# Heads' stage by a plan: when queries and keys are prepared and where the filling products stand

## The chip, the cores and the metric

The kernel runs on one core of a Trainium2 chip. The metric is the device time of one execution in microseconds (us). The engines are TensorE (PE; its weight loads are shown apart as PEld), VectorE (DVE), ScalarE (ACT), GpSimd (POOL) and SyncE (SP), whose queue issues the DMAs.

## The reference, cut to what matters

Two layers over 512 latent tokens and 256 context tokens of width 1024. The first mixes tokens by grouped-query attention with 16 heads of width 64 and 4 key/value heads; the second is a Mamba-2 mixer. Each is followed by a gated feed-forward network. The change touches the attention alone:

```python
q_l, k_l, v_l = jnp.split(h_lat @ w_qkv, [Q_DIM, Q_DIM + KV_DIM], axis=-1)
q_l = rms_norm(q_l.reshape(bsz, seq, N_HEADS, HEAD_DIM), q_norm)
k_l = rms_norm(k_l.reshape(bsz, seq, N_KV_HEADS, HEAD_DIM), k_norm)
q_l = apply_rope(q_l, cos, sin)
k_l = apply_rope(k_l, cos, sin)
...
s = jnp.einsum('bqhgd,bkhd->bhgqk', q, k).astype(jnp.float32) * (HEAD_DIM ** -0.5)
p = jax.nn.softmax(s, axis=-1).astype(v.dtype)
return jnp.einsum('bhgqk,bkhd->bqhgd', p, v)
```

Context queries see context keys only. `q`, `k` and `v` also exist for the context; there is no rotation for it. Besides, each layer has a modulation (shift, scale, gate) from a matrix product with the conditioning vectors.

## The kernel before

All of it is float32. Products of large matrices are made from a high and a low half of each operand: `split` casts the high half on ACT and subtracts on DVE or POOL for the low half, and `mm3` makes three products (high by high, high by low, low by high).

The attention goes through these stages. First the projections of keys and of the first four pairs' queries from slabs of weights (`ps_l`, `ps_c`). Then the *values' stretch*: `values()` makes the value products `ps_v`, 48 small steps. Between them stand the maxima of pair 0 and the preparation of pair 1's queries. Then the *heads' stage*: 16 heads in 8 pairs.

A pair (`class Pair`) has two parts. `maxima` multiplies queries by keys once for the row maxima (`ps_m`, reduced on DVE, `ma`, `mb`), and ends with their minima of the negated values `mz` and a diagonal `diag`. `steps` has seven steps: scores into `ps_s` (with the diagonal, which subtracts the maxima), an exponential on ACT into `pr`, a running sum on DVE (`acc`, `accc`). The value products `ps_o` and `ps_oc` come one step later, with the sum (`ps_sum`) and its reciprocal by logarithm and exponential (`final`). During the steps of a pair stands the `maxima` of the next. `ps_s` and `ps_m` share two buffers, so PE can run ahead of ACT and DVE by about a step.

A *preparation* (`normed`, in `queries` or `keys`) makes a pair's queries, or two key heads, ready. It squares and scales on ACT, sends four small DMAs that swap rows (`qsw`), rotates by three products on POOL (L534 to L536), sums columns on PE (`ssq`), makes a row scale on DVE and ACT (`rsa`, `rsy`, `rsu`, `rbq`), transposes it on PE (`rsTq`), multiplies it in on DVE (L540), and splits.

*Filling products* stand between the steps so that PE has work while the other engines follow. Those are the query projections of pairs 4 to 7 (`ps_q`), which a preparation follows, and six modulations (`ada`, `ps_ada`). `Fill.run` gives each step 1.75 us of them, from a list of generators in the order `123a4k5a6a7aaa` (digits: queries, with projection and preparation in one generator; k: the second keys; a: a modulation). After a `BREAK` a generator rests three steps and the next in the list goes on. What the next pair needs and isn't ready, `fill.require` forces at the pair's start. Weights are loaded when a generator starts. In pairs 6 and 7 the fill is the output projection (`ps_d`).

Each engine works its own queue in order. The program's order is not the queue's order in full: a scheduler places each instruction by its own estimate of when it is ready.

```python
adas = list(fill.q)
fill.q = [kgen if o == "k" else adas.pop(0) if o == "a" else qgen[int(o)] for o in "123a4k5a6a7aaa"]
...
    if p < 7:
        fill.require(qgen[p + 1])
        if p == 3:
            fill.require(kgen)
        m = pairs[p + 1].maxima()
    us = 1.75 if p < 6 else 2.9
```

Of the kernel before, what the change touches and what calls it, by code (L numbers as in the profile page):

```python
# [7 lines left out]
P = 128  # L8
F32 = mybir.dt.float32
F32R = mybir.dt.float32r  # L10
# [6 lines left out]
KT = D // P  # L17
L = 512
C = 256
# [48 lines left out]
def t3(g, name, dt=F32, n=T):  # L68
    return g.t3p.tile([P, n], dt, tag="t3", bufs=g.n3, name=name)


def t4(g, name, dt=F32):
    return g.p.tile([P, 1024], dt, tag="t4", bufs=10, name=name)


def _r(ap):

    return ap.bitcast(F32)


def split(g, src, hi, lo, lo_engine="dve", pin=False):

    nc = g.nc
    keep = g.tc.keep_in_program_order if pin else lambda i: i
    keep(nc.scalar.copy(hi, src))  # L85
    eng = nc.vector if lo_engine == "dve" else nc.gpsimd
    keep(eng.tensor_tensor(lo, src, _r(hi), ALU.subtract))  # L87


def load_w(g, dram, lo_engine="dve", pin=False):  # L90

    st = t4(g, "wst")
    wh = t4(g, "wh", F32R)
    wl = t4(g, "wl", F32R)
    g.nc.sync.dma_start(st, dram)
    split(g, st, wh, wl, lo_engine=lo_engine, pin=pin)
    return wh, wl


def mm3(g, w, outs, first, last):  # L100

    wh, wl = w
    mm = g.nc.tensor.matmul
    for out, (ah, al) in outs:
        mm(out, wh, ah, start=first, stop=False)  # L105
        mm(out, wh, al, start=False, stop=False)  # L106
    for out, (ah, al) in outs:
        mm(out, wl, ah, start=False, stop=last)  # L108
# [64 lines left out]
BREAK = object()  # L173
# [128 lines left out]
def S(g, name):  # L302
    return g.ps.tile([P, 1024], F32, tag="S", bufs=2, name=name)


def Bank(g, name):
    return g.ps.tile([P, 512], F32, tag="B", bufs=4, name=name)
# [72 lines left out]
def attention(g, fill, X, late):  # L380


    nc, I = g.nc, g.I
    S64 = slice(0, 64), slice(64, 128)
    Bk, Sb = (lambda name: Bank(g, name)), (lambda name: S(g, name))
    t2 = lambda name, dt=F32: g.t3p.tile([P, 512], dt, tag="t2", bufs=6, name=name)
    g.h = [[htiles(g, n, f"a{i}_{m}") for m in range(KT)] for i, n in enumerate((L, C))]
    hl, hc = g.h
# [58 lines left out]
    e = g.p.tile([P, 2 * KT], F32, name="silu")  # L447
# [8 lines left out]
    rsl, _, _ = next(norm)  # L456
# [12 lines left out]
    for m in range(KT):  # L469
# [14 lines left out]
        if m == 4:  # L484
            rsc = t3(g, "rsc", n=C)
            pt, _, _ = next(norm)
# [20 lines left out]
    raw = [t3(g, f"raw{j}") for j in range(6)]  # L507
# [18 lines left out]
    def normed(qs, gain, eng):  # L526

        sq = t3(g, "qsq")
        nc.scalar.activation(sq, qs, AF.Square)
        nc.scalar.activation(qs, qs, AF.Identity, scale=gain)  # L530
        sw = t2("qsw")
        for b in range(4):
            nc.sync.dma_start(sw[32 * (b ^ 1) : 32 * (b ^ 1) + 32], qs[32 * b : 32 * b + 32, :L])
        eng.tensor_tensor(qs[:, :L], qs[:, :L], g.cos, ALU.mult)  # L534
        eng.tensor_tensor(sw, sw, g.sin, ALU.mult)
        eng.tensor_tensor(qs[:, :L], qs[:, :L], sw, ALU.add)  # L536
        for r in rstd_rows(g, sq, T, g.blk, HD, "q", Bk):
            if r is not BREAK:
                pt, c0, c1 = r
                nc.vector.tensor_tensor(qs[:, c0:c1], qs[:, c0:c1], pt[:, : c1 - c0], ALU.mult)  # L540
            yield BREAK
# [3 lines left out]
    def keys(j, qs, eng):  # L545
        yield from normed(qs, kn, eng)
        nat = t3(g, f"kh{j}", F32R), t3(g, f"kl{j}", F32R)
        swp = t3(g, f"khs{j}", F32R), t3(g, f"kls{j}", F32R)
        split(g, qs, *nat)
        for a, b in zip(swp, nat):  # L550
            for e in range(2):
                nc.sync.dma_start(_r(a)[S64[e]], _r(b)[S64[1 - e]])
        k2[2 * j], k2[2 * j + 1] = (nat, swp), (swp, nat)
        yield 0

    qprep = {}

    def queries(p, qs, eng):
        if qs is None:
            w = load_w(g, I["wq"][p - 4], lo_engine="pool")  # L560
            yield BREAK
            qs = t3(g, "qs")
            for h, c0, n in ((hc, L, C), (hl, 0, L)):
                ps = Bk("ps_q")
                for k in range(KT):
                    ks = slice(k * P, (k + 1) * P)
                    mm3(g, (w[0][:, ks], w[1][:, ks]), [(ps[:, :n], h[k])], k == 0, k == KT - 1)
                    yield 3 * n / 2400
                nc.scalar.copy(qs[:, c0 : c0 + n], ps[:, :n])
            yield BREAK  # L570
        yield from normed(qs, g.qn8, eng)
        qprep[p] = t3(g, "qh", F32R), t3(g, "ql", F32R)
        split(g, qs, *qprep[p])
        yield 0
# [8 lines left out]
    class Pair:  # L583
# [43 lines left out]
        def steps(self):  # L627
# [61 lines left out]
                    lambda pr=pr, acc=acc: later_ctx(pr, acc))  # L689
            g.o.append(o)  # L690

    early = [keys(0, raw[0], nc.vector), queries(0, raw[1], nc.vector)]
    for n, j in enumerate((0, 1, 2, 4, 5, 3)):
        ps = Bk("ps_c")
        for k in range(KT):
# [7 lines left out]
    for gen in early:  # L703
        for _ in gen:
            next(vals)
            next(vals)
    qgen = {p: queries(p, raw[{1: 2, 2: 4, 3: 5}[p]] if p < 4 else None, nc.gpsimd) for p in range(1, 8)}
    kgen = keys(1, raw[3], nc.gpsimd)

    g.oT = []  # L710
# [2 lines left out]
    def osplit(p):  # L713
        hl_, hc_ = htiles(g, L, f"ol{p}"), htiles(g, C, f"oc{p}")
        o = g.o[p]
        if p < 6:
            o = t3(g, f"od{p}")
            nc.sync.dma_start(o, odram[p])
        split(g, o[:, :L], *hl_)
        split(g, o[:, L:T], *hc_)  # L720
        g.oT.append((hl_, hc_))

    adas = list(fill.q)
    fill.q = [kgen if o == "k" else adas.pop(0) if o == "a" else qgen[int(o)] for o in "123a4k5a6a7aaa"]
    g.o = []
    pairs = [Pair(p) for p in range(NH // 2)]

    m = pairs[0].maxima()
    for i, _ in enumerate(vals):
        if i % 5 == 2:  # L730
            next(m, None)
        if i % 6 == 5:
            next(qgen[1], None)
    for _ in m:
        pass
    late_step = None
    for p in range(NH // 2):
        m = iter(())
        if p < 7:
            fill.require(qgen[p + 1])  # L740
            if p == 3:
                fill.require(kgen)
            m = pairs[p + 1].maxima()
        us = 1.75 if p < 6 else 2.9
        for t, todo in enumerate(pairs[p].steps()):
            next(m, None)
            if late_step:
                late_step()
            late_step = todo
            if t == 0:  # L750
                if p == 6:
                    for i in range(5):
                        osplit(i)
                    late()
            if p == 7 and t == 3:
                osplit(5)
                osplit(6)
            fill.run(us)
    late_step()
    osplit(7)  # L760

# [490 lines left out]
def body(nc, tc, I, out, dbg=None):  # L1252
# [47 lines left out]
    def late():  # L1300
        for fs in ((0, 1, 2), (3, 4), (5, 6, 7))[:-1]:
            fill.add(project(fs))

    attention(g, fill, X, late)
    fill.drain()
    g.tables = True
# [133 lines left out]
```

## Time and profile before

| | |
|---|---|
| median of 3 runs | 1893.8 us (1892.28 to 1894.25) |
| profiled execution | 1893.6 us, span 1891.8 us, mean granted PE clock 0.997 |
| PE, DVE, ACT, POOL busy | 98%, 70%, 43%, 16% of the span |
| heads' stage, pairs 0 to 5 | from 107.8 to 295.6 us of the span |
| values' stretch | up to 107.8 us |

The profile's lines give start and length in us, the engine, the line in the code, the operation, what it writes and reads, and the shapes. In brackets stand the idle time before an instruction and the instruction that ended it. Matmuls are pipelined and their ends are modelled, so a busy PE is not yet a PE at full rate; the distance from one start to the next says more.

### The profile page before, as it was taken

What the parts mean: (1) busy time and instruction counts of PE and PEld (TensorE: products, weight loads), DVE (VectorE), ACT (ScalarE), POOL (GpSimd) and SP (SyncE); (2) the same over time, 40 slices, a digit from 0 to 9 for tenths busy, and PEclk for the clock granted to TensorE, in tenths of its full rate; (3) what the DMA queues carried; (4) which work ended last, traced back from release to release, by engine and by line L of the source; (5) the groups of instructions that cost most, each with busy time, mean ns of one, the idle gap of its engine ahead of it and who ended that gap; (6) DMA issues with size and microseconds to landing.
All of it is one profiled execution on the core that took longest, in us unless ns stands there. A gap on an engine that the chain in (4) does not pass through costs nothing.

```text
span 1891.8 us, 28789 instructions
## 1 busy us (share of the span) xinstructions
PE 1859.4 (98%) x11474; PEld 1548.3 (82%) x11474; DVE 1314.9 (70%) x1950; ACT 811.4 (43%) x1410; POOL 302.8 (16%) x266
## 2 busy tenths in 40 slices
PE   9999999999999999999999999999999999999999
PEld 7866565688888888888888888888887888888887
DVE  6587778687877776444487877777787476565655
ACT  4544443364222222222366676776666252323331
POOL 2231120040000000000041334444333210000000
PEclk9999999999999999999999999999999999999999
DMA  9322341115443553112224323333453222323232
GB/s 342 91 95 62 132 156 37 34 57 190 145 134 131 180 182 123 65 67 68 67 90 125 114 92 116 118 120 126 123 158 106 72 91 100 100 83 107 90 100 89
DMA packets 74070, 211.67 MB, mean 112 GB/s; under 512 B 9040, under 2 KB 14544, under 8 KB 73808
## 3 DMA queue, kind: packets, MB, share of 16 engines
q1 hardware_dynamic: 73936, 209.84, 33.5%
q8 instruction: 90, 1.47, 0.3%
q14 instruction: 44, 0.36, 0.1%
HBM read 198.79 MB, written 6.82 MB: 109 GB/s over the span
## 4 chain that ended last, share of the span: by engine, by line
PE 80%; DVE 11%; issue 3%; DMA 2%; ACT 2%; POOL 1%; SPq 0%; DVEq 0%; POOLq 0%; ACTq 0%
PE ps_up L108 10%; PE ps_up L106 10%; PE ps_up L105 10%; PE ps_d L105 6%; PE ps_d L106 6%; PE ps_d L108 6%; PE ps_in L108 4%; PE ps_in L106 4%; PE ps_in L105 4%; PE ps_o L636 2%; PE ps_s L672 2%; PE ps_st L1030 2%; DVE ht L281 1%; DVE wl L87 1%; PE ps_wo L108 1%
## 5 line engine op out<-in xcount | busy, mean ns | idle before, releaser
L87 DVE TENSOR_TENSOR wl<-wst,wh 128x1024 fp32r<-128x1024 f32 x207 | 260.4, 1258 | 229.3 <-PE ps_up L106 133.0
L85 ACT CAST wh<-wst 128x1024 fp32r<-128x1024 f32 x211 | 221.1, 1049 | 396.4 <-DMA wst<-in_wup 321.5
L106 PE MATMUL ps_up<-hlf,wh 128*128 128x512 f32 (+1 forms) x1008 | 357.0, 354 | 0.0
L108 PE MATMUL ps_up<-hhf,wl 128*128 128x512 f32 (+1 forms) x1008 | 356.8, 354 | 0.0
L105 PE MATMUL ps_up<-hhf,wh 128*128 128x512 f32 x1008 | 356.8, 354 | 0.0
L106 PEld LDWEIGHTS ps_up<-hlf,wh 128*128 128x128 f32 x1008 | 190.7, 189 | 26.3
L105 PEld LDWEIGHTS ps_up<-hhf,wh 128*128 128x128 f32 x1008 | 190.5, 189 | 26.5
L108 PEld LDWEIGHTS ps_up<-hhf,wl 128*128 128x128 f32 x1008 | 190.5, 189 | 26.3
L105 PE MATMUL ps_in<-hhs,wh 128*128 128x512 f32 (+1 forms) x560 | 204.4, 365 | 1.2 <-ACT dt L915 1.2
L106 PE MATMUL ps_in<-hls,wh 128*128 128x512 f32 (+1 forms) x560 | 199.4, 356 | 0.0
L108 PE MATMUL ps_in<-hhs,wl 128*128 128x512 f32 (+1 forms) x560 | 198.7, 355 | 0.0
L105 PE MATMUL ps_d<-hdh,wh 128*128 128x512 f32 (+1 forms) x568 | 193.5, 342 | 0.2 <-ACT hdh L85 0.2
L108 PE MATMUL ps_d<-hdh,wl 128*128 128x512 f32 (+1 forms) x568 | 193.5, 341 | 0.0
L106 PE MATMUL ps_d<-hdl,wh 128*128 128x512 f32 (+1 forms) x568 | 192.9, 340 | 0.3 <-DVE hdl L87 0.3
L781 DVE SCALAR_TENSOR_TENSOR X<-ps_d,mod,X 128x512 f32<-128x512 f32 (+1 forms) x224 | 124.8, 587 | 35.2 <-PE ps_d L108 35.0
L105 PEld LDWEIGHTS ps_in<-hhs,wh 128*128 128x128 f32 x560 | 105.9, 189 | 16.3 <-ACT dt L915 1.4
L106 PEld LDWEIGHTS ps_d<-hdl,wh 128*128 128x128 f32 x568 | 106.7, 188 | 14.8 <-DVE hdl L87 0.7
L108 PEld LDWEIGHTS ps_in<-hhs,wl 128*128 128x128 f32 x560 | 105.8, 189 | 14.8
L108 PEld LDWEIGHTS ps_d<-hdh,wl 128*128 128x128 f32 x568 | 106.7, 188 | 13.1
L105 PEld LDWEIGHTS ps_d<-hdh,wh 128*128 128x128 f32 x568 | 106.3, 188 | 13.6 <-ACT hdh L85 0.7
L106 PEld LDWEIGHTS ps_in<-hls,wh 128*128 128x128 f32 x560 | 106.0, 189 | 13.2
L675 ACT ACTIVATE pr<-ps_s 128x1024 f32<-128x1024 f32 x56 | 57.2, 1022 | 108.8 <-PE ps_s L674 106.5
(344 smaller groups left out, 3682.8 us busy)
## 6 DMA issues: line engine op xcount, KB each, us to landing
wst<-in_wup SPq DMA_DIRECT2D x88, 512.0 KB, 3.3
wada<-in_adaT SPq DMA_DIRECT2D x56, 512.0 KB, 3.3
wst<-in_win SPq DMA_DIRECT2D x48, 512.0 KB, 3.4
wst<-in_wdown SPq DMA_DIRECT2D x44, 512.0 KB, 3.9
E<-ad SPq DMA_DIRECT2D x64, 256.0 KB, 6.4
wada<-in_adaB SPq DMA_DIRECT2D x24, 512.0 KB, 4.0
ec<-ead SPq DMA_DIRECT2D x64, 128.0 KB, 5.1
wst<-in_wout SPq DMA_DIRECT2D x16, 512.0 KB, 3.3
```

What stands on the lines that cost most here:

```text
L85: keep(nc.scalar.copy(hi, src))
L87: keep(eng.tensor_tensor(lo, src, _r(hi), ALU.subtract))
L105: mm(out, wh, ah, start=first, stop=False)
L106: mm(out, wh, al, start=False, stop=False)
L108: mm(out, wl, ah, start=False, stop=last)
L281: nc.vector.scalar_tensor_tensor(t[:, c0:c1], ap, g.moda[layer][ca][:, m, v : v + 1], rs[:, c0:c1], ALU.mult, ALU.mult)
L636: nc.tensor.matmul(po[S64[e], :n], v, pr[:, 512 * e + off : 512 * e + off + n], start=first, stop=last)
L672: nc.tensor.matmul(outs[e], kk[e][a][S64[e], k], b[S64[e], q], start=i == 0, stop=False)
L675: nc.scalar.activation(pr, ps, AF.Exp)
L781: nc.vector.scalar_tensor_tensor(ap, o[:, c0:c1], gate[:, m, v : v + 1], ap, ALU.mult, ALU.add)
L1030: nc.tensor.matmul(ps[:, d * 256 : (d + 1) * 256], Bt[:, t * P : (t + 1) * P], xw[d][t], start=t == ts[0], stop=t == ts[-1])
```

## The change

The heads' stage is laid out by a plan. Projection (`qproj`) and preparation (`queries`) of a pair's queries are now two generators. One preparation is done in each pair of heads: `prep` = queries of pair 3, second keys, queries of pairs 4 to 7, at least a pair ahead of their use, at fixed steps (0, 3, 4, 5, rest at 6). Pairs and steps count from 0. The third queries, those of pair 2, are prepared in the values' stretch, beside pair 1's. The fill comes from one stream, `a4a567aaaa`, in shares of 1.04 us a step, with the DMA of an item sent two items ahead and the split of its weights one item ahead. A modulation's rest follows two steps after its products. From pair 6 on nothing is changed.

```diff
-    def queries(p, qs, eng):
-        if qs is None:
-            w = load_w(g, I["wq"][p - 4], lo_engine="pool")
-            yield BREAK
-            qs = t3(g, "qs")
...
+    def qproj(p):
+        st = t4(g, "wst")
+        nc.sync.dma_start(st, I["wq"][p - 4])
+        yield
+        w = t4(g, "wh", F32R), t4(g, "wl", F32R)
+        split(g, st, *w, lo_engine="pool")
+        yield
+        qs = qraw[p] = t3(g, "qs")
...
+    def queries(p, eng):
+        qs = qraw[p]
         yield from normed(qs, g.qn8, eng)
...
-    fill.q = [kgen if o == "k" else adas.pop(0) if o == "a" else qgen[int(o)] for o in "123a4k5a6a7aaa"]
+    items = [adas.pop(0) if o == "a" else qproj(int(o)) for o in "a4a567aaaa"]
+    tails = []
+    def stream():
+        for it in items[:2]:
+            next(it)
+        yield
+        for i, it in enumerate(items):
+            if i + 2 < len(items):
+                next(items[i + 2])
+            if i + 1 < len(items) and i + 1 in (1, 3, 4, 5):
+                next(items[i + 1])
+            if i in (1, 3, 4, 5):
+                yield from it
+            else:
+                next(it)
+                tails.append([2, it])
+                yield 1.95
...
+    prep = {0: qgen[3], 1: kgen, 2: qgen[4], 3: qgen[5], 4: qgen[6], 5: qgen[7]}
...
         if i % 6 == 5:
             next(qgen[1], None)
+        if i in (12, 26, 30, 34):
+            next(qgen[2], None)
+        if i == 20:
+            next(side)
...
-            fill.run(us)
+            if p < 6:
+                if t in (0, 3, 4, 5):
+                    next(prep[p])
+                if t == 6:
+                    for _ in prep[p]:
+                        pass
+                spread(1.04)
+            else:
+                fill.run(2.9)
```

What it moves, at three places. PE in pair 0, from its first maxima on, before:

```order
L236 MATMUL ssq<-cst,qsq 128x2 x6
L672 MATMUL ps_s<-qh,kh_1139 128x512
...
L600 MATMUL ps_m<-khs_1141,qh 128x512
L236 MATMUL ssq<-cst,qsq 128x2 x6
L636 MATMUL ps_o<-pr,v_910 64x512 x2
L129 MATMUL ps_ada<-wada,sc_83 32x128 x32
```

and after:

```order
L236 MATMUL ssq<-cst,qsq 128x2 x6
L129 MATMUL ps_ada<-wada,sc_83 32x128 x32
L680 MATMUL ps_s<-qh,kh_1139 128x512
...
L608 MATMUL ps_m<-khs_1141,qh 128x512
L644 MATMUL ps_o<-pr,v_910 64x512 x2
L105 MATMUL ps_q<-hha_0_118,wh 128x256
L106 MATMUL ps_q<-hla_0_119,wh 128x256
L108 MATMUL ps_q<-hha_0_118,wl 128x256
```

One preparation's column sums stand there in place of two, and the query products start in the second step.

POOL at the same place (`raw4` and `raw5` are the raw queries of pairs 2 and 3, `raw3` the second keys, `wl` a low half of query weights), before:

```order
L87 TENSOR_TENSOR wl_1571<-wst_1569,wh_1570 128x1024
L536 TENSOR_TENSOR raw4_902<-raw4_902,qsw_1454 128x512
L87 TENSOR_TENSOR wl_1623<-wst_1621,wh_1622 128x1024
L534 TENSOR_TENSOR raw5_903<-raw5_903,cs_74 128x512
L535 TENSOR_TENSOR qsw_1482<-qsw_1482,cs_74 128x512
L536 TENSOR_TENSOR raw5_903<-raw5_903,qsw_1482 128x512
L534 TENSOR_TENSOR raw3_901<-raw3_901,cs_74 128x512
```

and after:

```order
L534 TENSOR_TENSOR raw5_903<-raw5_903,cs_74 128x512
L535 TENSOR_TENSOR qsw_1506<-qsw_1506,cs_74 128x512
L536 TENSOR_TENSOR raw5_903<-raw5_903,qsw_1506 128x512
L87 TENSOR_TENSOR wl_1540<-wst_1351,wh_1539 128x1024
L87 TENSOR_TENSOR wl_1893<-wst_1597,wh_1892 128x1024
L87 TENSOR_TENSOR wl_1983<-wst_1890,wh_1982 128x1024
L534 TENSOR_TENSOR raw3_901<-raw3_901,cs_74 128x512
```

Three low halves now stand in a row ahead of the second keys' rotation; before, the third came after it.

PE in pair 5, from its first value products (before) and from its first preparation product (after). Before:

```order
L636 MATMUL ps_o<-pr,v_910 64x512 x2
L129 MATMUL ps_ada<-wada,sc_83 32x128 x32
...
L636 MATMUL ps_o<-pr,v_911 64x512 x2
L236 MATMUL ssq<-cst,qsq 128x2 x6
...
L636 MATMUL ps_o<-pr,v_913 64x512 x2
L253 MATMUL rsTq<-cst,rbq 128x128 x4
```

and after:

```order
L236 MATMUL ssq<-cst,qsq 128x2 x6
L129 MATMUL ps_ada<-wada,sc_83 32x128 x32
...
L644 MATMUL ps_o<-pr,v_911 64x512 x2
L129 MATMUL ps_ada<-wada,sc_83 32x128 x32
...
L644 MATMUL ps_o<-pr,v_912 64x512 x2
L253 MATMUL rsTq<-cst,rbq 128x128 x4
L129 MATMUL ps_ada<-wada,sc_83 32x128 x32
```

The last preparation's column sums move ahead by two steps, and three modulations, of which two stood together at the pair's start, are spread to steps 0, 2 and 3. The last three steps hold no modulation in either.

More of the change, by code (lines that the diff above doesn't have):

```diff
@@ L556, in attention @@
     qprep = {}
-    def queries(p, qs, eng):
-        if qs is None:
-            w = load_w(g, I["wq"][p - 4], lo_engine="pool")
-            yield BREAK
-            qs = t3(g, "qs")
[L563 to L570, printed above, removed]
+    qraw = {p: raw[j] for p, j in ((0, 1), (1, 2), (2, 4), (3, 5))}
+    def qproj(p):
[6 more added lines that the diff above has]
+        qs = qraw[p] = t3(g, "qs")
+        for h, c0, n in ((hc, L, C), (hl, 0, L)):
+            ps = Bk("ps_q")
+            for k in range(KT):
+                ks = slice(k * P, (k + 1) * P)
+                mm3(g, (w[0][:, ks], w[1][:, ks]), [(ps[:, :n], h[k])], k == 0, k == KT - 1)
+                yield 3 * n / 2400
+            nc.scalar.copy(qs[:, c0 : c0 + n], ps[:, :n])
+    def queries(p, eng):
+        qs = qraw[p]
         yield from normed(qs, g.qn8, eng)
@@ L690, in steps @@
             g.o.append(o)
-    early = [keys(0, raw[0], nc.vector), queries(0, raw[1], nc.vector)]
+    early = [keys(0, raw[0], nc.vector), queries(0, nc.vector)]
     for n, j in enumerate((0, 1, 2, 4, 5, 3)):
@@ L706, in attention @@
             next(vals)
-    qgen = {p: queries(p, raw[{1: 2, 2: 4, 3: 5}[p]] if p < 4 else None, nc.gpsimd) for p in range(1, 8)}
+    qgen = {p: queries(p, nc.gpsimd) for p in range(1, 8)}
     kgen = keys(1, raw[3], nc.gpsimd)
@@ L721, in osplit, with spread @@
         g.oT.append((hl_, hc_))
-    adas = list(fill.q)
-    fill.q = [kgen if o == "k" else adas.pop(0) if o == "a" else qgen[int(o)] for o in "123a4k5a6a7aaa"]
+    adas, fill.q = list(fill.q), []
+    items = [adas.pop(0) if o == "a" else qproj(int(o)) for o in "a4a567aaaa"]
[15 more added lines that the diff above has]
+                yield 1.95
+    def spread(us):
+        nonlocal owed
+        for e in list(tails):
+            e[0] -= 1
+            if e[0] == 0:
+                for _ in e[1]:
+                    pass
+                tails.remove(e)
+        owed += us
+        while owed > 0:
+            r = next(side, None)
+            if r is None:
+                return
+            owed -= r
+    owed, side = 0.0, stream()
+    prep = {0: qgen[3], 1: kgen, 2: qgen[4], 3: qgen[5], 4: qgen[6], 5: qgen[7]}
     g.o = []
@@ L733, in attention @@
             next(qgen[1], None)
-    for _ in m:
-        pass
+        if i in (12, 26, 30, 34):
+            next(qgen[2], None)
+        if i == 20:
+            next(side)
+    for gen in (m, qgen[1], qgen[2]):
+        for _ in gen:
+            pass
     late_step = None
@@ L739, in attention @@
         if p < 7:
-            fill.require(qgen[p + 1])
-            if p == 3:
-                fill.require(kgen)
             m = pairs[p + 1].maxima()
-        us = 1.75 if p < 6 else 2.9
+        if p == 6:
+            for _ in side:
+                pass
+            for _, gen in tails:
+                for _ in gen:
+                    pass
         for t, todo in enumerate(pairs[p].steps()):
@@ L757, in attention @@
                 osplit(6)
-            fill.run(us)
+            if p < 6:
[3 more added lines that the diff above has]
+                    for _ in prep[p]:
+                        pass
+                spread(1.04)
+            else:
+                fill.run(2.9)
     late_step()
```

## Prediction

> **What bounds the kernel now.** I read the page first, then the heads' stage cut into its pairs, then TensorE's (PE's) rows in order of time, then the rows of the other engines where PE stood still.
>
> ```profile
> span 1891.8 us, 28789 instructions
> PE 1859.4 (98%) x11474; PEld 1548.3 (82%) x11474; DVE 1314.9 (70%) x1950; ACT 811.4 (43%) x1410; POOL 302.8 (16%) x266
> ```
>
> PE is busy 98% of the span, so a change of order gains only what PE loses now. The stage's six pairs that the change re-orders, each from its first score product to the next pair's (stretch, length, then busy us and instructions of PE, its weight loads, VectorE = DVE, ScalarE = ACT, GpSimd = POOL; PE's granted clock, DMA share, GB/s):
>
> ```profile
> 107.80:141.10 33.30, 29.48 (x247) 18.72 (x246) 28.99 (x36) 14.83 (x23) 16.57 (x11) 0.95 0.34 109
> 141.10:170.87 29.77, 29.63 (x192) 18.16 (x191) 22.64 (x31) 12.55 (x16) 6.95 (x4) 1.00 0.18 58
> 170.87:204.03 33.16, 31.27 (x299) 18.88 (x298) 26.18 (x41) 15.23 (x23) 2.38 (x1) 1.00 0.38 118
> 204.03:232.93 28.90, 28.90 (x182) 16.83 (x179) 22.08 (x33) 10.31 (x13) 5.01 (x3) 1.00 0.28 95
> 232.93:262.88 29.95, 29.70 (x192) 18.02 (x191) 22.07 (x32) 12.29 (x18) 5.44 (x3) 1.00 0.28 92
> 262.88:295.57 32.69, 29.86 (x335) 17.11 (x334) 29.14 (x41) 15.48 (x20) 4.99 (x3) 0.95 0.53 178
> ```
>
> Pairs 0, 2 and 5 are long. In 0 and 5 DVE is busy 29 us and PE's granted clock is 0.95. Busy PE is not yet PE at full rate, so I price each unit of PE's work by start-to-start distances where nothing is late:
>
> ```profile
> 137.80 1.08 PE L636 MATMUL ps_o<-pr,v 128*64 128x512 f32 x4
> ...
> 139.66 0.44 PE L253 MATMUL rsTq<-cst,rbq 128*128 128x128 f32 x2
> 139.86 0.36 PE L105 MATMUL ps_q<-hha,wh 128*128 128x256 f32 x1
> ...
> 141.10 0.49 PE L672 MATMUL ps_s<-qh,kh 64*128 64x512 f32 x1
> ...
> 142.13 0.27 PE L600 MATMUL ps_m<-kh,qh 64*128 64x256 f32 x1
> ...
> 142.46 1.08 PE L636 MATMUL ps_oc<-pr,v 128*64 128x256 f32 x8
> ...
> 143.91 0.44 PE L253 MATMUL rsTq<-cst,rbq 128*128 128x128 f32 x2
> 144.11 0.48 PE L105 MATMUL ps_q<-hha,wh 128*128 128x512 f32 x1
> ...
> 144.98 0.49 PE L672 MATMUL ps_s<-qh,kh 64*128 64x512 f32 x1
> ...
> 150.97 1.08 PE L636 MATMUL ps_o<-pr,v 128*64 128x512 f32 x4
> 151.98 0.50 PE L105 MATMUL ps_q<-hha,wh 128*128 128x512 f32 x1
> ...
> 154.27 0.49 PE L672 MATMUL ps_s<-qh,kh 64*128 64x512 f32 x1
> ```
>
> Scores 1.03 us, maxima 0.33, values 1.01, the last values with their sum 1.86, context values with their sum 1.45, transposes 0.20 for two (0.41 for four). Nine query products of 512 columns take 2.29 and three 0.87: 0.237 each and 0.16 for a block of them; nine of 256 take 1.24. A preparation's column sums and one modulation (ada):
>
> ```profile
> 109.16 1.50 PE L236 MATMUL ssq<-cst,qsq 128*128 128x2 f32 x12
> 110.59 0.50 PE L672 MATMUL ps_s<-qh,kh 64*128 64x512 f32 x1
> 114.58 1.95 PE L129 MATMUL ps_ada<-wada,sc 128*32 128x128 f32 x64
> 116.47 0.50 PE L672 MATMUL ps_s<-qh,kh 64*128 64x512 f32 x1
> ```
>
> 1.43 and 1.88. Counting each pair's units at these prices gives its content, and the rest of its length is stall: content 26.9, 29.6, 30.4, 28.0, 29.2, 25.6; stall 6.4, 0.1, 2.8, 0.9, 0.7, 7.1. Together 169.7 and 18.0 us. The 18.0 is what can be won. Its causes:
>
> ```profile
> 126.53 0.50 PE L600 MATMUL ps_m<-kh,qh 64*128 64x512 f32 x1 [1.46 <-DVE mb L602]
> 195.06 1.04 ACT L85 CAST wh<-wst 128x1024 fp32r<-128x1024 f32 x1 [3.33 <-DMA wst<-in_wq]
> 197.09 0.38 PE L672 MATMUL ps_s<-qh,khs 64*128 64x256 f32 x1 [1.72 <-ACT pr L675]
> 112.84 2.35 POOL L87 TENSOR_TENSOR wl<-wst,wh 128x1024 fp32r<-128x1024 f32 x1
> 112.94 3.07 DVE L247 SCALAR_TENSOR_TENSOR rbq<-rsu,rsy 128x768 f32<-128x768 f32 x1
> 166.00 1.29 POOL L534 TENSOR_TENSOR qs<-qs,cs 128x512 f32<-128x512 f32 x1 [5.68 <-DMA qsw<-qs]
> 118.67 0.96 DVE L247 SCALAR_TENSOR_TENSOR rbq<-rsu,rsy 128x768 f32<-128x768 f32 x1
> 281.00:290.00 9.00, 6.73 (x34) 3.19 (x32) 9.00 (x10) 2.96 (x4) 3.48 (x2) 0.81 0.44 170
> ```
>
> Pair 0 holds most of three preparations, and PE waits for DVE's maxima, whose turn comes late. POOL lengthens that: the same DVE operation takes 3.07 us against a POOL subtraction and 0.96 alone. In pair 2 ACT stands at the high half of the last query weights, whose DMA has not landed; the exponentials queue behind it and PE with them. In pair 5 the fill is spent early and DVE is full (9.00 of 9.00 us).
>
> **The change, part by part.** *Third queries into the values' stretch.* Their 1.43 + 0.61 = 2.0 us of PE work leave pair 0 and enter the stretch, where nothing covers PE: net 0. There a late row scale can hold PE; 0 is one end, and a wait like the 1.46 for maxima the other. I take 0.3, nearer the lower: that wait came where DVE had most of three preparations, and the stretch now gets two.
>
> *Even filling.* Query products stand in 30 blocks for 25, at 0.16 each: +0.8. The products themselves are the same. The row under this is 2.29 against 0.87. [...]
>
> With one preparation less and the blocks, content becomes 27.8, 28.4, 29.6, 28.6, 28.6, 25.9 = 168.9 (pair 0: seven scores 7.2, seven maxima 2.3, six values with the sum 6.9, one preparation 2.0, one ada 1.9, fill 24 products of 256 and 15 of 512 in six blocks 7.4).
>
> *One preparation per pair.* Pairs 3 and 4 already look so: DVE 22 of 29 us, POOL 5, stall 0.9 and 0.7. Pairs 1 to 4 should be like them; bounds 0.1 (pair 1 now) and 2.5 each. I take 0.7, 0.6, 0.8 and 0.9. Pair 0 loses most of two preparations on DVE and 3 x 1.29 us of rotation for each on POOL, and keeps two low halves of weights on POOL (2.35 each). So it comes near pairs 3 and 4 in load, with POOL still busier; between 0.1 and 3 (half its stall) I take 1.0.
>
> *Weights early.* Three weight tiles are fetched before pair 0's middle, their high halves cast in pairs 0 and 1. ACT's wait of 3.33 and PE's of 1.72 in pair 2 go; nothing is late next there, since DVE has 7 us to spare. The third low half stands ahead of the second keys' rotation on POOL and needs pair 4's query products done (a buffer): these end in step 1 of pair 1, and DVE asks for the rotation's result in step 3. Steps 2 and 3 hold 4.3 and 2.8 us of PE work, against 2.35 + 3 x 1.29 = 6.2 of POOL. That fits by 0.9 us, and pair 1's 0.7 covers a miss of that size.
>
> *Pair 5* keeps its modulations, the last preparation and the output weights' low halves on DVE. Off go the remaining two scalings of pair 6's queries and their low half, done in pair 4; on comes one more low half:
>
> ```profile
> 264.93 0.68 DVE L540 TENSOR_TENSOR qs<-qs,rsTq 128x512 f32<-128x512 f32 x1
> ...
> 267.62 0.96 DVE L87 TENSOR_TENSOR ql<-qs,qh 128x768 fp32r<-128x768 f32 x1
> 275.75 1.23 DVE L87 TENSOR_TENSOR wl<-wst,wh 128x1024 fp32r<-128x1024 f32 x1 [1.33 <-ACT wh L85]
> ```
>
> The second scaling is half as wide, an estimated 0.4. So 29.1 - (0.7 + 0.4 + 1.0) + 1.2 = 28.2 us of DVE. Without an idle moment that leaves a stall of 28.2 - 25.9 = 2.3; with as much idle DVE as now (32.7 - 29.1 = 3.6) it is 5.9. I take 5.0, nearer the upper, because the order still ends the pair with two steps and a boundary without fill.
>
> *The sum.* Stalls 1.0 + 0.7 + 0.6 + 0.8 + 0.9 + 5.0 = 9.0 for 18.0: -9.0. Content in the pairs -0.8, in the values' stretch +2.0 + 0.3. Together -7.5. Pairs 6 and 7 and all behind them keep their order of work. The profiled execution took 1893.6 us (span 1891.8), 0.2 below the median of the runs, so 1886.1 against it.
>
> **Rivals.** (a) *Nothing measurable* (under 0.2%, 3.8 us, about what a measurement can tell): pair 5 stays at 7 and pair 0 at 3, since DVE is what is short there and the work on it is the same. -7.5 + 2 + 2 = -3.5: 1890. For it: DVE's 29 us in both pairs. Against it: pair 0 really loses two preparations.
>
> (b) *Slower: the rotation meets the diagonal.* At a pair's end DVE must do this chain before PE's next scores can close (pair 1's end; the last row is the same operation in pair 4):
>
> ```profile
> 167.22 1.23 DVE L602 TENSOR_REDUCE mb<-ps_m 128x4 f32<-128x1024 f32 x1 [2.12 <-PE ps_m L600]
> 168.37 0.71 DVE L686 TENSOR_TENSOR accc<-pr 128x512 f32<-128x512 f32 x1
> 169.00 1.76 DVE L618 TENSOR_TENSOR mz<-ma,mb 64x6 f32<-64x6 f32 x4
> 171.00 1.03 DVE L623 TENSOR_TENSOR diag<-id,mz 128x384 fp32r<-128x384 f32 x2
> 262.06 0.69 DVE L618 TENSOR_TENSOR mz<-ma,mb 64x6 f32<-64x6 f32 x4
> ```
>
> Undisturbed it is 1.2 + 0.7 + 0.7 + 1.0 = 3.6 us, and PE covers 1.86 of values and sum, about 1.2 of fill and 0.8 of scores, 3.9. If POOL's three rotation operations (3.9) fall on that chain, the boundary loses 3.6: over five pairs 18 where I have 4, so 1886 + 14 = 1900. It decides if the first rotation operation starts inside the last step in more than two of the five. For it: in pair 1 it fell there (166.00 above), and the minima took 1.76 for 0.69. Against it: that boundary lost under 0.6 (pair 1's stall is 0.1, and pair 2 has the rest). [...]
>
> (c) *More:* pair 5 at its lower end and pair 0 at 0.1, 2.7 + 0.9 better, and pairs 1 to 4 at 0.3 each, 1.8 better: -12.9, 1881. For it: a PE that is not halted keeps its clock (0.81 in the worst stretch).
>
> (d) *ACT blocked again:* the output weights' casts in pair 5 wait for DMAs that wait for buffers; one such block costs 1.7 to 3.3, which leaves 1888 to 1889. I count it within my forecast.
>
> **How the numbers follow.** My forecast (1883 to 1889.5) 0.60, (a) 0.20, (b) 0.08, (c) 0.12. Faster holds mine and (c) and a little of (a): 0.74; same 0.18; slower 0.08. The range reaches from (c) into (a): 1880.5 to 1891.5.
>
> **What would show it.** Pair lengths near 29, 29, 30, 29, 30, 31; no ACT wait for query weights; PE's clock 1.00 in pair 0; the values' stretch 2.3 longer; DVE still full at the end of pair 5. I am wrong if pair 0 waits for pair 4's low half of weights, if boundaries show diagonals waited for, or if pair 5 stays at 32.7.

## The result and the profile after

The changed kernel took 1886.5 us (median of 6 runs, 1885.32 to 1888.97), the one before beside it 1894.03 (1891.67 to 1894.77). The ratio is 0.9961, with a 95% interval of 0.9951 to 0.9971: 5.5 to 9.3 us faster. The forecast was 1886.1. The profiled execution shown here is the slowest of the six, 1888.97 us. The page:

```profile
span 1887.2 us, 28798 instructions
PE 1857.0 (98%) x11474; PEld 1549.0 (82%) x11474; DVE 1315.0 (70%) x1950; ACT 811.3 (43%) x1410; POOL 303.5 (16%) x266
```

Every engine is busy for the same time as before, to 0.3%, in the same number of instructions; left to change are the waits, the spacing of PE's products and its clock. The values' stretch and pairs 0 to 6 of the changed kernel, cut as in the prediction (stretch, length, busy us and instructions of PE, weight loads, DVE, ACT, POOL; PE's granted clock, DMA share, GB/s):

```profile
85.53:111.56 26.03, 25.87 (x202) 23.16 (x200) 19.88 (x29) 10.18 (x19) 7.56 (x6) 1.00 0.41 127
111.56:143.07 31.51, 29.63 (x234) 18.27 (x233) 24.22 (x29) 13.85 (x18) 9.25 (x5) 0.95 0.34 112
143.07:171.56 28.49, 28.49 (x243) 17.69 (x242) 23.77 (x35) 12.51 (x18) 8.10 (x4) 1.00 0.37 121
171.56:201.17 29.61, 29.61 (x191) 18.15 (x190) 23.65 (x36) 13.16 (x20) 7.13 (x4) 1.00 0.17 58
201.17:229.67 28.50, 28.50 (x185) 17.29 (x184) 23.09 (x33) 13.51 (x19) 4.77 (x3) 1.00 0.21 66
229.67:258.26 28.59, 28.59 (x234) 17.20 (x233) 22.03 (x32) 11.32 (x17) 4.98 (x3) 1.00 0.26 84
258.26:288.52 30.26, 26.64 (x338) 16.25 (x336) 27.96 (x44) 14.33 (x18) 4.80 (x3) 1.00 0.71 253
288.52:336.74 48.22, 46.65 (x252) 29.83 (x251) 37.72 (x62) 16.29 (x26) 0.00 (x0) 0.96 0.05 17
```

The same two stretches of the kernel before that the prediction did not show, the values' stretch and pair 6:

```profile
84.24:107.80 23.56, 23.56 (x184) 21.12 (x182) 14.37 (x22) 8.29 (x15) 4.84 (x4) 1.00 0.37 119
295.57:340.71 45.14, 44.33 (x251) 28.78 (x250) 37.54 (x62) 16.78 (x27) 0.00 (x0) 1.00 0.09 30
```

In pairs 1 to 4 PE is busy for their whole length. Pair 0 is 1.8 us shorter and still holds a wait. Pair 5 is 2.4 shorter, and pair 6, which the prediction left alone, 3.1 longer. From the first values' product to pair 7's first score product the stage takes 251.2 us; before it took 256.5.

**Pair 0** waits where the prediction said it would be wrong: at pair 4's low half of weights. PE's rows and POOL's, the number in brackets being the idle time before the row and what ended it:

```profile
118.81 0.28 PE L106 MATMUL ps_q<-hla,wh 128*128 128x256 f32 x1
120.97 0.39 PE L108 MATMUL ps_q<-hha,wl 128*128 128x256 f32 x1 [1.88 <-POOL wl L87]
122.88 1.98 PE L644 MATMUL ps_o<-pr,v 128*64 128x512 f32 x4
...
113.94 1.28 POOL L534 TENSOR_TENSOR raw<-raw,cs 128x512 f32<-128x512 f32 x1 [13.03 <-ACT pr L683]
...
116.55 2.07 POOL L536 TENSOR_TENSOR raw<-raw,qsw 128x512 f32<-128x512 f32 x1
118.58 2.34 POOL L87 TENSOR_TENSOR wl<-wst,wh 128x1024 fp32r<-128x1024 f32 x1
```

POOL takes the low half behind pair 3's rotation, and that rotation began only at 113.94, late for the products. The wait costs more than its 1.88 us: 1.9 us later the values' products take 1.98 us instead of 1.08. The reason is the granted clock (columns as above):

```profile
118.60:121.80 3.20, 1.32 (x9) 0.94 (x9) 3.20 (x3) 0.11 (x1) 2.32 (x2) 1.00 0.71 278
121.80:122.60 0.80, 0.80 (x8) 0.44 (x6) 0.20 (x1) 0.80 (x1) 0.00 (x0) 0.85 0.05 20
...
123.40:124.20 0.80, 0.80 (x4) 0.00 (x0) 0.80 (x2) 0.26 (x1) 0.80 (x1) 0.50 0.03 10
...
125.00:125.80 0.80, 0.80 (x5) 0.80 (x6) 0.80 (x1) 0.00 (x0) 0.22 (x1) 0.52 0.00 0
```

For 3.41 us (0.50 from 122.36 to 125.77) PE has half its clock, which loses 1.7 us. Such half-clock stretches come in all the traces, in this size or two or three in a row, and each total has to be read with them. The kernel before has two of them in the stage as well, in pairs 0 and 5 (columns as above):

```profile
130.00:133.40 3.40, 1.94 (x6) 0.48 (x6) 3.40 (x4) 0.81 (x1) 2.07 (x2) 0.74 0.00 0
133.40:136.80 3.40, 3.40 (x23) 2.69 (x23) 2.69 (x3) 0.00 (x0) 0.00 (x0) 0.76 0.00 0
...
286.00:290.00 4.00, 3.87 (x20) 2.13 (x18) 4.00 (x5) 0.65 (x1) 0.00 (x0) 0.67 0.01 4
```

**Pairs 5 and 6.** DVE, ACT and PE at pair 5's end:

```profile
283.02 0.42 DVE L540 TENSOR_TENSOR qs<-qs,rsTq 128x256 f32<-128x256 f32 x1
...
289.35 0.69 DVE L626 TENSOR_TENSOR mz<-ma,mb 64x6 f32<-64x6 f32 x4
290.07 1.23 DVE L87 TENSOR_TENSOR wl<-wst,wh 128x1024 fp32r<-128x1024 f32 x1
291.21 1.02 DVE L631 TENSOR_TENSOR diag<-id,mz 128x384 fp32r<-128x384 f32 x2
...
273.93 1.05 ACT L85 CAST wh<-wst 128x1024 fp32r<-128x1024 f32 x1 [3.83 <-DMA wst<-in_w_o]
...
283.46 0.83 ACT L85 CAST qh<-qs 128x768 fp32r<-128x768 f32 x1 [2.67 <-DVE qs L540]
284.20 1.02 ACT L683 ACTIVATE pr<-ps_s 128x1024 f32<-128x1024 f32 x1
...
285.27 0.38 PE L680 MATMUL ps_s<-qh,kh 64*128 64x256 f32 x1 [1.74 <-ACT pr L683]
...
292.29 0.50 PE L682 MATMUL ps_s<-diag,onesr 64*128 64x512 f32 x2 [1.57 <-DVE diag L631]
```

DVE works without an idle moment from 275 us on. Its late scaling of the last queries (283.02) holds ACT's cast of them (283.46), the exponential queues behind the cast (284.20), and PE waits 1.74 us for it. Then a low half of output weights stands on DVE between the minima and the diagonal, and pair 6 opens with a wait for that diagonal. It is the fourth such low half; the kernel before had three ahead of the diagonal and the fourth behind it:

```profile
296.02 0.69 DVE L618 TENSOR_TENSOR mz<-ma,mb 64x6 f32<-64x6 f32 x4
...
297.35 1.02 DVE L623 TENSOR_TENSOR diag<-id,mz 128x384 fp32r<-128x384 f32 x2
...
302.21 1.22 DVE L87 TENSOR_TENSOR wl<-wst,wh 128x1024 fp32r<-128x1024 f32 x1
```

### The profile page after: what moved, and what is told of

The parts are those of the page before. It is cut to its first block, busy times and chain, and to the rows that moved or that the text cites. A ratio compares the mean times of both kernels' runs of the same rounds, so it can differ in the third digit from the quotient of the medians.

```text
span 1887.2 us, 28798 instructions
## 1 busy us (share of the span) xinstructions
PE 1857.0 (98%) x11474; PEld 1549.0 (82%) x11474; DVE 1315.0 (70%) x1950; ACT 811.3 (43%) x1410; POOL 303.5 (16%) x266
## 4 chain that ended last, share of the span: by engine, by line
PE 80%; DVE 11%; issue 4%; POOL 2%; ACT 2%; DMA 1%; SPq 0%; DVEq 0%; POOLq 0%; ACTq 0%
PE ps_up L106 10%; PE ps_up L108 10%; PE ps_up L105 10%; PE ps_d L105 6%; PE ps_d L106 6%; PE ps_d L108 6%; PE ps_in L108 4%; PE ps_in L106 4%; PE ps_in L105 4%; PE ps_s L680 2%; PE ps_o L644 2%; PE ps_st L1090 1%; DVE wl L87 1%; DVE ht L281 1%; DVE xf L1020 1%
```

## The experiments

Execution times of one kernel spread over 2 to 13 us here, so the stage is compared in the traces as well: from the first values' product to pair 7's first score product, and pairs 5 and 6 together. "Half" counts the half-clock stretches inside the stage. Times are medians, the kernel before ran on the same chip beside each, and the ratio is given as its 95% interval.

The granted clock of each run is known too. (1 - clock) x span is what a run lost to half clock; within one kernel's runs the time rises by some 0.7 us for each us of it (150 runs, correlation 0.75). "Net" is an estimate from this: the gain in mean time over the kernel before beside it, with 0.69 of the loss taken off both. Its standard error is 0.4 to 1.1 us.

| kernel | us | before | ratio | stage | pairs 5+6 | half | net |
|---|---|---|---|---|---|---|---|
| before | 1894.0 | | | 256.5 | 77.8 | 2 | |
| changed | 1886.5 | 1894.0 | 0.9951–0.9971 | 251.2 | 78.5 | 2 | |
| again | 1887.5 | 1895.7 | 0.9941–0.9968 | 249.9 | 77.2 | 2 | 6.5 |
| early4 | 1888.5 | 1895.7 | 0.9943–0.9971 | 247.4 | 76.9 | 1 | 7.7 |
| lumpy | 1896.9 | 1895.7 | 0.9995–1.0022 | 257.9 | 68.3 | 2 | -2.5 |
| third0 | 1886.4 | 1895.7 | 0.9937–0.9965 | 248.2 | 77.2 | 1 | 6.7 |
| b_third | 1890.0 | 1893.3 | 0.9972–0.9991 | 252.6 | 74.0 | 0 | 0.9 |
| b_early | 1890.0 | 1893.3 | 0.9971–0.9990 | 252.7 | 77.3 | 2 | 2.5 |
| wopool_e4 | 1887.8 | 1893.3 | 0.9953–0.9982 | 249.5 | 79.6 | 3 | 5.9 |
| wonolo_e4 | 1879.6 | 1893.3 | 0.9906–0.9934 | 243.0 | 71.8 | 1 | 12.5 |
| woe1 | 1885.8 | 1895.6 | 0.9927–0.9956 | 248.3 | 77.1 | 1 | 7.3 |
| woe2 | 1890.5 | 1895.6 | 0.9962–0.9986 | 251.8 | 80.5 | 3 | 4.2 |
| pin34 | 1884.4 | 1892.6 | 0.9949–0.9976 | 248.4 | 77.2 | 3 | 6.8 |
| woe1_pin | 1885.0 | 1892.6 | 0.9948–0.9974 | 247.0 | 75.7 | 2 | 6.7 |

**again**: the changed kernel, unedited.

> The changed kernel once more, for a second trace and for runs beside the others. If its losses come from its order, pair 0 again stalls 3.8 us with PE behind POOL's low half of pair 4's query weights, and pair 6 again opens with some 5 us of stall behind the diagonal; 1885 to 1889 us. The rival is that the 1.3 us by which the values' stretch began later in the first trace, and the wait in pair 6, are chance: then the stretch begins at 84.2 us as in the kernel before (85.5 in the first trace), and pair 6 is near 45 us (48.2 there).

The values' stretch, pair 0, pair 5 and pair 6 of the second trace:

```profile
84.28:110.40 26.12, 25.88 (x203) 23.16 (x201) 19.96 (x29) 10.19 (x19) 7.58 (x6) 1.00 0.39 125
110.40:141.92 31.52, 29.63 (x235) 18.03 (x234) 24.49 (x29) 13.85 (x18) 9.27 (x5) 0.95 0.33 112
257.03:289.07 32.04, 28.23 (x336) 17.05 (x334) 28.69 (x50) 14.33 (x18) 4.74 (x3) 0.95 0.66 235
289.07:334.22 45.15, 45.15 (x253) 29.15 (x251) 35.88 (x56) 16.30 (x26) 0.00 (x0) 1.00 0.06 18
```

Pair 0 repeats to 0.01 us, so its loss belongs to the order. The 1.3 us by which the first trace began its values' stretch late is chance, as the rival said: nothing was changed ahead of it, and over the 14 traces the stretch begins anywhere from 84.0 to 85.5 us. Pair 6 is at 45.15, again as the rival had it, but the loss isn't gone: pair 5 is 1.8 longer. The half-clock stretch fell behind the border in one trace and before it in the other, and PE, later by it, then had no wait for the diagonal where the first trace has 1.57 us. Only the sum of the two pairs can be compared: 78.5 and 77.2, against 77.8 before, with one half-clock stretch in each of the three. There the change won nothing.

**early4**: pair 4's low half ahead of pair 3's rotation.

```diff
+        if i == 32:
+            next(items[1])          # in the values' stretch
...
-            if i + 1 < len(items) and i + 1 in (1, 3, 4, 5):
+            if i + 1 < len(items) and i + 1 in (3, 4, 5):
```

> Pair 4's query weights are split in the values' stretch, so that POOL takes their low half before the last rotation and not behind it. Theory: PE's wait of 1.9 us and the lower clock behind it go, pair 0's stall falls from 3.8 to about 1.0, and the kernel is 2.8 us below the changed one: 1883.7 against 1886.5. Rival one: DVE's maxima are late next, the stall only falls to 2.5: 1885.2. Rival two: the low half (2.3 us of POOL) now excludes DVE's scalings in the stretch, which grows by 1 or more: 1885 to 1887.

```profile
108.81 2.50 POOL L87 TENSOR_TENSOR wl<-wst,wh 128x1024 fp32r<-128x1024 f32 x1 [7.80 <-PE ps_v L521]
111.96 1.26 POOL L534 TENSOR_TENSOR raw<-raw,cs 128x512 f32<-128x512 f32 x1 [0.65 <-DMA qsw<-raw]
...
110.16:139.86 29.70, 28.20 (x234) 17.67 (x233) 22.82 (x29) 12.91 (x17) 7.34 (x5) 1.00 0.40 134
```

The wait and the half clock behind it are gone, pair 0 falls from 31.52 to 29.70, the stage by 2.6 against again. The six further kernels below with this early split have no wait of PE for POOL there either; pair 0 takes 28.9 to 30.3 in them, five of the six with a half-clock stretch from about 114 us on. That shows the cause. The medians do not show it (1888.5 beside 1887.5): early4's runs lost more to half clock (8.7 us on average, again's 6.0), in the profiled execution 3.4 us of it in two stretches between 419 and 426 us, outside the changed code. Net of the clock early4 is 1.2 better, which is within the error. Of the stall 2.0 is left, between theory and the first rival, and not for that rival's reason: the longest wait left, 1.1 us, is for an exponential.

**lumpy**: `spread(1.75)` instead of `spread(1.04)`.

> The filling products are handed out at 1.75 us a step, as the kernel before did, and not at 1.04; all else is as in the changed kernel. They then end in pair 3 (43.7 us / 1.75 = 25 steps), and pairs 4 and 5 have none. Theory (even filling pays, since DVE's chain in each step needs cover): pair 4's stall rises from 0 to about 4, pair 5's from 4.7 to about 9, less 0.8 for fewer blocks: +7.5, 1894. Rival: the stalls are DVE's total load at the end of the stage, which filling does not change: within 1.5 us of the changed kernel, 1885 to 1888.

Pairs 3, 4 and 5:

```profile
217.18:246.09 28.91, 25.50 (x274) 14.35 (x270) 26.65 (x38) 14.53 (x18) 4.18 (x3) 1.00 0.53 191
246.09:274.48 28.39, 23.75 (x144) 11.95 (x142) 25.10 (x39) 12.73 (x17) 5.67 (x3) 0.94 0.10 28
274.48:298.05 23.57, 21.11 (x145) 10.92 (x143) 20.94 (x29) 10.75 (x15) 6.32 (x3) 1.00 0.32 106
```

The stage is 8.0 us longer than in again, near the theory's 7.5, and the kernel no faster than the one before. The places differ from the theory's: at the prediction's prices pair 3 stalls 5.2 us, pair 4 8.5 and pair 5 3.6. Pair 4 without filling takes 28.4 us, of which 1.7 go to a half-clock stretch, and with 8.7 us of it 28.6: filling there costs 0.2 us, or 1.9 without the clock. With the filling spent early, one preparation per pair and early weights together bring nothing (257.9 against 256.5). But lumpy spends it earlier than the kernel before did, which still had 48 query products in pair 4 and three modulations in pair 5.

**third0**: the third queries' preparation back in pair 0.

```diff
-        if i in (12, 26, 30, 34):
-            next(qgen[2], None)
...
+                for gen in (qgen[2], prep[0]) if p == 0 else (prep[p],):
```

> The third queries' preparation is put back into pair 0, beside the fourth's; the weights' low half then comes early on POOL, as in the kernel with the early split, which is the one to compare with. Theory (two preparations crowd DVE in pair 0): the stretch is 2.4 us shorter, pair 0 has 2.0 us more of PE work and 1 to 3 us more of stall: +1 to +3 against the early split, 1885 to 1887. Rival (pair 0's whole gain came from this move): stall 6.5 as in the kernel before, +5, 1889. Rival (nothing gained by the move): 0, 1884.

Against early4 the stage is 0.8 longer (248.2 and 247.4), below the theory's 1 to 3 and near the rival's nothing. Against again it is 1.8 shorter: taking the move back puts the low half early on POOL (at 115.52 us, ahead of the fourth queries' rotation), and PE has no wait for it. So the third queries' move gained little, and in the form of the change it lost more through POOL's order. By their times the three kernels are not told apart.

**b_third**: the kernel before, with the same move alone.

```diff
+        if i in (12, 26, 30, 34):
+            next(qgen[2], None)
```

> The kernel before with one part of the change alone: the third queries' preparation goes into the values' stretch; the rest of pair 0's fill, the lumpy filling and the late weights stay. Measured from the first values' product to pair 7 (256.5 us before). Theory (three preparations crowd DVE in pair 0, and the third costs more than the second): stretch +2.4, pair 0 33.3 less 2.0 of work and less about 3.5 of stall, 27.8; the stage 253.4, the kernel 3 below the one before. Rival (as putting it back cost only 0.8): the stage 255.7, no difference in time.

The stage falls by 3.9 and the time by about 3, but not as the theory had it: pair 0 stays at 33.1. Its fill budget draws the next items of the queue forward, so the gain appears in pair 2 (33.2 to 29.8) and pair 5 (32.7 to 27.4), and 1.4 each is given back in pairs 4 and 6. And 3.4 of the 3.9 are the two half-clock stretches of the trace before, of which this trace has none in the stage. The runs say the same: they lost 3.1 us to half clock on average, those of the kernel before beside them 6.2, and net of it 0.9 is left. The number was right, the mechanism wrong, and the rival (no difference) nearer to what the order itself gained.

**b_early**: the kernel before, with the weights' fetch one tile ahead.

```diff
-            w = load_w(g, I["wq"][p - 4], lo_engine="pool")
+            if p == 4:
+                wst[4] = fetch(4)
+            if p < 7:
+                wst[p + 1] = fetch(p + 1)      # the DMA alone
+            w = t4(g, "wh", F32R), t4(g, "wl", F32R)
+            split(g, wst[p], *w, lo_engine="pool")
```

> The kernel before with another part alone: the fetch of each query weight tile is issued one tile ahead, its cast and low half stay where they were. Theory (pair 2's stall is ACT's wait of 3.3 us for that transfer): pair 2 from 33.2 to 30.9, all other pairs as before; the stage 254.2, the kernel 2.3 below the one before. Rival (something else is late next in pair 2, or the buffer taken longer delays a modulation's weights): within 1 us of 256.5.

Among the waits of ACT and of PE in pairs 0 to 2 of the kernel before (total us, times, longest) stand these two. The same view of the kernel with the early fetch has no wait of ACT for a transfer, and none of PE for an exponential:

```profile
ACT wh L85 <- DMA wst<-in_wq: 5.3, 2, 3.3
...
PE ps_s L672 <- ACT pr L675: 2.2, 2, 1.7
```

Pair 2 fell by 1.2 (33.2 to 31.9; 2.3 expected) and pair 0 by 1.9, which was not expected: there too a cast had waited for its transfer (2.0 us at 128.1). The part alone is worth 3.8 in the stage, with two half-clock stretches in both traces, and net of the clock 2.5 in the time.

**wopool_e4 and wonolo_e4**: early4, and the low halves of five tiles of output weights on POOL (`load_w(..., lo_engine="pool")` in `project`), or left out (`ws.append((wh, wh))`), so that its result is no longer the layer's.

> The changed kernel with the early split of pair 4's weights, and with the low halves of the first five tiles of output weights on POOL. Compare pairs 5 and 6 with the early split alone (76.9 us together) and with the kernel before (77.8). Theory (DVE's load bounds the end of pair 5): four or five low halves of 1.2 us leave DVE there; 73 to 74, and the kernel 3 us under the early split: 1882 to 1885. Rival (POOL's 2.3 us each exclude DVE's sums, which were 2.3 us instead of 1.2 under POOL): no gain or up to 2 us worse, 77 to 79.

> As the early split, but the low halves of the first five tiles of output weights are left out altogether (their products read the high half twice), so neither DVE nor POOL has that work. Theory (DVE's load bounds the end of pair 5): pairs 5 and 6 go from 76.9 to 72 to 73. Rival (the chain from scores over exponentials to values, or ACT's casts that wait for these weights' transfers, bounds it): not below 76.

Pairs 5 and 6 without the low halves; then, with them on POOL, POOL and DVE in pair 5:

```profile
255.24:282.23 26.99, 26.28 (x336) 16.22 (x334) 24.29 (x41) 15.08 (x19) 4.81 (x3) 1.00 0.79 278
282.23:327.03 44.80, 43.34 (x252) 28.73 (x250) 38.12 (x63) 17.17 (x27) 0.00 (x0) 1.00 0.16 58
```

```profile
271.94 5.71 POOL L87 TENSOR_TENSOR wl<-wst,wh 128x1024 fp32r<-128x1024 f32 x2 [0.58 <-ACT wh L85]
278.74 2.35 POOL L87 TENSOR_TENSOR wl<-wst,wh 128x1024 fp32r<-128x1024 f32 x1 [1.09 <-ACT wh L85]
...
272.82 2.59 DVE L690 TENSOR_TENSOR acc<-acc,pr 128x1024 f32<-128x1024 f32 x1 [1.42 <-ACT pr L683]
...
278.93 3.25 DVE L690 TENSOR_TENSOR acc<-acc,pr 128x1024 f32<-128x1024 f32 x1
```

Without that work pairs 5 and 6 take 71.8, 5.1 us less (1.7 of it a half-clock stretch that early4 had there), and the kernel 1879.6: DVE's load is what bounds pair 5's end. On POOL the pairs take 79.6, with two half-clock stretches more than early4; even less these 3.4 us it wins 0.7 at most. The sums on DVE take 2.59 and 3.25 us instead of 1.22 while POOL subtracts. A reduction kept its time (1.21 us, where the mean of its kind in the stage is 1.22) in the changed kernel during the subtraction that POOL began at 118.58:

```profile
118.57 1.21 DVE L610 TENSOR_REDUCE ma<-ps_m 128x2 f32<-128x1024 f32 x1
119.70 2.30 DVE L688 TENSOR_TENSOR acc<-pr 128x1024 f32<-128x1024 f32 x1
```

The sum that began during this subtraction ended at 122.00, 1.08 us behind the subtraction's own end at 120.92, and so took 2.30 us instead of 1.22.

**woe1 and woe2**: early4, and one or two tiles of output weights fetched and split in pair 4.

```diff
+            if (p, t) in [(4, 0)]:              # woe2: [(4, 0), (4, 4)]
+                g.wo([(4, 0)].index((p, t)))    # load_w of that tile, kept for project()
```

> The early split, and the first tile of output weights is fetched and split at pair 4's first step, where DVE has 7 of 28.6 us free, not in pair 5. Theory (DVE's load bounds the end of pair 5; leaving out all five low halves gave -5.1): one low half of 1.2 us less there, pairs 5 and 6 from 76.9 to 75.7, pair 4 unchanged at 28.6; the kernel 1.2 under the early split's stage (247.4 from the first values' product to pair 7). Rival (the three buffers held through pairs 4 and 5 delay the modulations' weights, two of which then wait): pairs 5 and 6 at 77 to 80.

> The same with two tiles of output weights, at pair 4's first and fifth step. Theory (DVE's load): 2.4 us less in pair 5, pairs 5 and 6 at 74.5, the stage 245; the kernel near 1882 where the changed kernel's runs had 1886 to 1888. Rival (buffers): four of the ten are then held by output weights, the modulations' transfers wait and PE with them: pairs 5 and 6 at 77 to 80, or pair 4 longer than 28.6.

One tile: 77.1, no change in the sum, though early4 had a half-clock stretch there and woe1 has none. The low half left pair 5, but DVE then stood idle for a cast whose transfer came later:

```profile
276.41 1.23 DVE L87 TENSOR_TENSOR wl<-wst,wh 128x1024 fp32r<-128x1024 f32 x1 [1.81 <-ACT wh L85]
```

Two tiles: 80.5, in the rival's range, but 3.4 of it are two half-clock stretches, and PE waited only 0.5 us for modulations' weights. That the buffers are the cause is not shown. Pair 4 kept its 28.6 us in both.

**pin34 and woe1_pin**: `pin=f > 2` in `project`'s `load_w`, on early4 and on woe1, so that the fourth low half comes after the diagonal.

> The early split, and the fourth and fifth tile of output weights are kept in written order, so that the fourth low half (1.23 us on DVE, right ahead of pair 6's diagonal in the early split) comes only after pair 6 has begun. Theory (DVE's queue ahead of that diagonal sets when pair 6 closes its first scores): pairs 5 and 6 from 76.9 to 75.7, the stage 246.2 from the first values' product to pair 7, and the kernel some 4 us under the changed one, 1883 against 1887 on the same chip. Rival (the pair's end is held by ACT's casts or by the clock after the earlier waits): within 0.5 of 76.9. Rival (the weights now come late for pair 6's or 7's filling products): the stage's gain is given back behind pair 7's start, the span behind it longer than 1551.

> The same, and the first tile of output weights fetched and split in pair 4, so that two low halves are left on DVE in pair 5 ahead of the diagonal, where the early split has four. Theory (DVE's load): pairs 5 and 6 from 77.05 (the kernel with the early tile alone, three low halves) to 75.8 or, with ACT's later transfer no longer in the way, 74.5. Rival (in that kernel DVE waited 1.8 us for a cast that waited for the weights' transfer, so the transfers bound it): no better than the pinned one without the early tile.

pin34 has 77.2 and not 75.7: the low half is gone from ahead of the diagonal, but pair 5 drew two half-clock stretches where early4 drew one. woe1_pin has 75.7, with one. If 1.7 us is taken off for each, early4 has 75.2, pin34 73.8, woe1_pin 74.0 and woe1, which had none there, 77.1. By this reckoning the pin is worth 1.4 to 3.0 and the theory of DVE's load holds; by the sums as they stand it is worth nothing to 1.3. The weights did not come too late: behind pair 7's start the span is 1551.9 us in pin34 and 1550.6 in woe1_pin, 1551.5 in again. One wait stayed at 1.7 us in early4, woe1, pin34 and woe1_pin: PE for the exponential that stands behind the cast of the last queries. It is gone in wonolo_e4 only. To place that cast behind the exponential was not tried.

Of the versions that change the changed kernel and compute everything, only lumpy is told apart from it by its interval; by the stage woe1_pin is the shortest of them, 3.0 us under again, and net of the clock the two are level within the error.

## Why the prediction was right, and where it was not

The forecast of the time was right: 1886.1 against 1886.5, a gain of 7.5 against 7.5, in the forecast's own range. That it is right to 0.4 us is luck, as its parts show:

| term | forecast | trace 1 | again |
|---|---|---|---|
| values' stretch, longer by | 2.3 | 2.5 | 2.6 |
| pair 0 | 28.8 | 31.5 | 31.5 |
| pairs 1 to 4 together | 118.2 | 115.2 | 115.1 |
| pairs 5 and 6 together | 76.0 | 78.5 | 77.2 |
| stage, shorter by | 7.6 | 5.3 | 6.5 |

The forecast lengths are the prediction's contents plus its stalls, with pair 6 at its 45.1 of before.

- *Third queries in the stretch*: sized right (2.3, measured 2.5 and 2.6).
- *Even filling*: blocks went from 25 to 30 as forecast. That the later pairs need filling is shown by lumpy (+8.0). The prediction named it only as a cost of 0.8 and as one reason for pair 5.
- *Pair 0* was mis-sized: stall 3.8 at the prediction's prices, where it took 1.0, and a granted clock of 0.95 where it had 1.00. The step that failed is the low halves of weights: they were counted as load on POOL (2.35 us each), not by their place in its queue. The prediction had written this wait down as the thing that would prove it wrong, and early4 shows it as the cause: 1.8 us back in pair 0, 2.6 in the stage.
- *Two preparations out of pair 0* as the source of its gain is not borne out. Moving the third one alone did not shorten pair 0 (b_third, where other fill came in its place), and moving it back cost 0.8 in the stage (third0). At the prediction's prices pair 0 stalls 2.2 us with two preparations (third0) and 2.0 with one (early4).
- *Weights early*: right in its mechanism, undersized. ACT's wait in pair 2 is gone; the part alone gives 3.8 in the stage, in pair 0 as well as in pair 2, where the prediction had only pair 2. One wait of ACT for query weights is left in the changed kernel's pair 0, against the prediction's sign (3.2 us at 121.69, 3.8 in again), and PE had no wait for ACT from it.
- *Pairs 1 to 4* were better than forecast: at its prices a stall of 0.2 us is left in pair 1 and none in the others, for 0.7, 0.6, 0.8 and 0.9. Rival (c) had 0.3 each for them. Of their ends PE waited for a diagonal at pair 4's alone, 0.7 us, so rival (b)'s case (more than two of five ends) did not occur.
- *Pairs 5 and 6*: the step "pairs 6 and 7 and all behind them keep their order of work" failed. Pair 5's 4.7 of stall in the first trace (its content is 25.6 by count, not 25.9) looks like the forecast's 5.0, but the rest of it had moved over the border, where the diagonal waits behind a fourth low half. In again pair 5 stalls 6.5. The sum gained nothing, which is rival (a)'s case for pair 5; the reason that rival gave, DVE being short there, is shown by wonolo_e4.
- *Clock*: the prediction counted as stall all that its prices left over. In the trace before 3.4 of the 18.0 us were two half-clock stretches, which no term of the sum names; rival (c) has the clock as a reason for a larger gain. In the changed kernel's trace pairs 1 to 4, where PE is busy for their whole length, have 1.00, and pair 0 with its wait has 0.95.

So two errors of opposite sign cancelled: pairs 1 to 4 gave 3.0 more, and pairs 0, 5 and 6 gave 3.9 to 5.2 less. The traces account for 5.3 to 6.5 us, the medians for 7.5; outside the stage the two profiled spans agree within 0.7 (1635.3 and 1636.0). The rest is within the interval of the ratio (5.5 to 9.3), and the clock can make it up: the changed kernel's runs lost 5.3 us on average to half clock and again's 6.0, those of the kernel before 6.2 to 8.9 in the four sets beside the experiments. Beside again, where the mean gain was 8.4, it is 6.5 net of the clock, which is what the traces give. So some 2 us of the gain are an estimate of what fewer half-clock stretches bring, a term that the forecast didn't have. For the first set the clock of the kernel before is known for one run only.

## What to carry to other kernels

Price a moved operation by what it stands behind on its engine's queue, not only by its load: the same subtraction cost PE a wait of 1.9 us behind a rotation's three operations (2.34 us long, changed kernel) and none ahead of them (2.50 us long, early4). Where an engine is full up to the end of a stage, sum the stall over the border, since what a pair gains may only show up in the next one (pair 5 took 30.3 and 32.0 us in the changed kernel's two traces, pair 6 48.2 and 45.2). Don't spend the filling products early: pairs 4 and 5, left without them, stalled by 8.5 and 3.6 us, and that ate the gain of all other parts (lumpy), though the early fetch had gained by itself without even filling (b_early). Count the half-clock stretches before two traces or two times are compared: 3.4 of b_third's 3.9 us were theirs.

## What was not expected of the hardware

The granted clock of PE falls to 0.50 for 3.4 us soon after PE stood still for a time far shorter than that, in the stage mostly 1.5 to 1.9 us (1.88 at 119.1 and 1.57 at 290.7 in the changed kernel), and values' products take 1.98 us instead of 1.08 (at 122.88 there). It does not follow from a wait with certainty: woe1 had waits of 1.7 and 1.6 us at pair 5's end and kept its full clock, pin34 had two such stretches in a row. So one order of work gives times apart by an estimated 1.7 us, what 3.41 us at half clock lose, or by a multiple of it.

The traces' clock records show more. The half-clock stretches of one trace begin on one grid of 3.41 us: in the changed kernel at 20.0, 122.4 and 293.0 us, 30 and 50 steps apart. Counted on this grid over the 14 traces, 27 windows held 1.6 us or more without a PE product, and 26 of them were followed by half clock (the exception is the wait at 283.5 us in the changed kernel); of 71 windows with 1.1 to 1.6 us 15 were, and of some 7600 with less, 8. Both of woe1's waits lie across a border of the grid (281.5 and 288.4 us), so that no window held 1.6 us. Where the borders fall is not set by the program: in the changed kernel's two traces the grid stands 1.5 us apart, counted from the start of the span. What sets the grid, no run shows.
